# A hybrid mLSTM and DeltaNet decoder step: the scheduler plays the program with instruction times

## Chip, cores and metric

The kernel runs on one core of one Trainium2 chip. The metric is the device time of one execution in microseconds (us). TensorE, VectorE, ScalarE, GpSimd and SyncE each work through a queue of their own in order; the profile calls them PE, DVE, ACT, POOL and SP, and PEld is TensorE loading weights.

## What is computed

Two layers, each a token mixer and a dense MLP, both followed by a layer norm over `ALPHA * x + sublayer(x)`. The first mixer is an mLSTM, the second a gated DeltaNet. There is one new sequence of 512 tokens and 8 samples of 4 tokens, which start from given states; model width 1024, MLP width 4096.

```python
# mLSTM, per chunk of the sequence and head
s = einsum(q, k) * w_intra
num = s @ v + w_inter * (q @ C);  den = s.sum() + w_inter * (q @ n)
h = num / max(abs(den), exp(-m_t))
C = decay * C + einsum(w_k, k, v)
out = (sigmoid(o) * head_rms(h)) @ w_out
...
# gated DeltaNet: A = I + strict(kb k^T * decay), sol = A^-1 [v*beta, kb*exp(G)] = [u, w]
v_new = u - w @ S
o = qg @ S + attn @ v_new
S = gL * S + kdec^T @ v_new
out = (head_rms(o) * silu(z)) @ w_out
...
# MLP
square(relu(x @ w1)) @ w2
```

The state S runs through the chunks of the prompt, so a chunk's step needs the state that the chunk before it left.

## The kernel before

All activations lie transposed: features on the 128 partitions, the 512 + 32 = 544 tokens along the free axis, in two halves of 272. Every large product goes through `mm3` (its matmul is L194): float32 is emulated by three passes, hi*hi, hi*lo and lo*hi. A weight tile of 512 KB comes by a DMA on SyncE's queue (`wraw`), ScalarE copies it to the high part `wh` (L111) and VectorE subtracts for the low part `wl` (L112); there are two buffers of each. PSUM has banks under four tags: g (3, the projections), a (2), s (2, the recurrent steps) and t (1).

Work in the two mixers is cut into units of two heads. In the mLSTM a unit is projected (L194), scanned over four chunks of 128 tokens (`scan`: transposes and scores L742, L743; L757, L759 for the outputs; L762 for the state; `head_out` on VectorE and ScalarE, L706 to L722, normalises the heads; L735 transposes them), and per pair of units the samples are decoded (`decode`: L786 to L821, where L821 is 16 passes a unit, then L824 and the state updates L834). `gate_out` and `out` close a pair.

In the DeltaNet a unit is projected, prepared (L1075 to L1098), its triangular matrix inverted in small blocks (`invert`, L1163 to L1210, with blocks of VectorE's L1124 and L1126 in front), and scanned over four chunks. One chunk of `scan` is a chain: L1253 (state times keys and queries) on TensorE, L1256 on VectorE, L1264 on TensorE, L1266 on VectorE and L1268 on ScalarE, L1271 and L1280 on TensorE, L1274 and L1282 on VectorE, then `norm_heads` (L1225 to L1229) on ScalarE and VectorE, and L1242 transposes the result. `decode` (L1311 to L1396; L1367 multiplies by the samples' states) and `update` (L1411 and L1417 on GpSimd, L1424 on TensorE) do the samples; `gate_out` makes the gate `sgmz` (L1438), `out` projects.

The program is written as Python generators. In the DeltaNet three lanes (inversion, scan, decode with update) are advanced by one step after so many L194 passes of the projection, as the table PERIODS says, in the order of ORDER; in the mLSTM the order is ORDER_A.

```python
HP = 400
AHEAD = 300
ORDER_A = "p0 s0 p1 s1 d0 y0 p2 s2 p3 s3 w0 d1 y1 w1"
ORDER = "p0 p1 p2 p3 y0 w0 p4 p5 y1 w1 p6 p7 y2 w2 y3 w3"
PERIODS = {"p0": (3, 3, 4), "y0": (5, 5, 6), "p7": (3, 3, 6)}
```

The order in which the program is written is a priority and not yet the order on an engine. The tile framework's scheduler plays the program through: at each point it gives an engine, out of the instructions whose operands and buffers are ready in that play, the one with the highest priority. Weight loads are written as if they stood 300 instructions earlier (AHEAD, L184), the mLSTM's scan and decode 400 (HP, L869, L872). The order that comes out is fixed when the kernel is built; on the chip each engine follows it and waits on semaphores. It is set up in `kernel`:

## Time and profile before

| | us |
|---|---|
| median of 3 runs | 1852.68 |
| lowest, highest | 1843.46, 1853.33 |
| profiled execution, its own time | 1849.81 |
| its span, first to last instruction | 1847.9 |
| TensorE busy | 1764.1 (95%) |
| VectorE busy | 1033.4 (56%) |
| ScalarE busy | 830.8 (45%) |
| GpSimd busy | 221.8 (12%) |
| mean granted TensorE clock | 0.961 |

The mLSTM mixer lies at about 0 to 340 us, the first MLP at 350 to 690, the DeltaNet at 690 to 1455, the second MLP behind it. [...] A matmul that waits for a semaphore at the head of the queue can be inside another's modelled time, so busy is not the same as useful: in a stretch the number of passes tells more.

### The profile page before, as it was taken

What the parts mean: (1) busy time and instruction counts of PE and PEld (TensorE: products, weight loads), DVE (VectorE), ACT (ScalarE), POOL (GpSimd) and SP (SyncE); (2) the same over time, 40 slices, a digit from 0 to 9 for tenths busy, and PEclk for the clock granted to TensorE, in tenths of its full rate; (3) what the DMA queues carried; (4) which work ended last, traced back from release to release, by engine and by line L of the source; (5) the groups of instructions that cost most, each with busy time, mean ns of one, the idle gap of its engine ahead of it and who ended that gap; (6) DMA issues with size and microseconds to landing.
All of it is one profiled execution on the core that took longest, in us unless ns stands there. A gap on an engine that the chain in (4) does not pass through costs nothing.

```text
span 1847.9 us, 35864 instructions
## 1 busy us (share of the span) xinstructions
PE 1764.1 (95%) x14580; PEld 1693.1 (92%) x14580; DVE 1033.4 (56%) x2360; ACT 830.8 (45%) x1874; POOL 221.8 (12%) x441
## 2 busy tenths in 40 slices
PE   7999999999999999899899999999899999999997
PEld 7999998999999998889788989898799899999996
DVE  7554766432344377775763777576458643234436
ACT  6444355421243157665542764475245642134314
POOL 2000000000000001223515322511240000000000
PEclk9999999999999999898987999999689999999999
DMA  4131222222223221222413423331233222222321
GB/s 158 58 106 67 75 81 92 84 88 92 85 87 103 85 69 51 67 54 84 141 37 108 117 75 102 111 94 53 77 98 101 80 82 91 92 82 91 105 68 49
DMA packets 84293, 158.89 MB, mean 86 GB/s; under 512 B 37536, under 2 KB 41504, under 8 KB 83616
## 3 DMA queue, kind: packets, MB, share of 16 engines
q1 hardware_dynamic: 84128, 156.60, 27.3%
q8 instruction: 115, 1.88, 0.4%
q14 instruction: 50, 0.41, 0.1%
HBM read 140.51 MB, written 16.06 MB: 85 GB/s over the span
## 4 chain that ended last, share of the span: by engine, by line
PE 79%; DVE 9%; ACT 4%; DMA 3%; POOL 3%; issue 2%; SPq 0%; ACTq 0%; DVEq 0%; POOLq 0%
PE pg_t L194 38%; PE pm_s L194 12%; PE pm_a L194 12%; PE pm_s L1367 2%; POOL sst L1417 1%; PE pm_s L1424 1%; DVE lnt L380 1%; DVE lnt L381 1%; PE pm_a L1089 1%; PE pm_s L1253 1%; PE pm_s L1264 1%; PE pm_s L1271 1%; ACT wh L111 1%; DVE wl L112 1%; DVE XL L392 1%
## 5 line engine op out<-in xcount | busy, mean ns | idle before, releaser
L194 PE MATMUL pg_t<-XH,wh 128*128 128x272 f32 x1480 | 444.8, 301 | 7.2 <-DVE sgmz L1438 5.0
L112 DVE TENSOR_TENSOR wl<-wraw,wh 128x1024 fp32r<-128x1024 f32 x200 | 245.1, 1225 | 368.6 <-ACT wh L111 367.1
L194 PE MATMUL pg_t<-XH,wl 128*128 128x272 f32 x1480 | 438.6, 297 | 0.8 <-DVE wl L112 0.8
L194 PE MATMUL pg_t<-XL,wh 128*128 128x272 f32 x1480 | 438.4, 296 | 0.0
L111 ACT CAST wh<-wraw 128x1024 fp32r<-128x1024 f32 (+1 forms) x201 | 210.0, 1045 | 495.3 <-PE pg_t L194 245.4
L194 PEld LDWEIGHTS pg_t<-XH,wh 128*128 128x128 f32 x1480 | 285.6, 193 | 12.3 <-DVE sgmz L1438 5.9
L194 PEld LDWEIGHTS pg_t<-XL,wh 128*128 128x128 f32 x1480 | 285.6, 193 | 2.3
L194 PEld LDWEIGHTS pg_t<-XH,wl 128*128 128x128 f32 x1480 | 284.9, 193 | 2.8 <-DVE wl L112 1.7
L194 PE MATMUL pg_t<-h,wh 128*128 128x272 f32 x672 | 129.1, 289 | 0.0
L194 PEld LDWEIGHTS pg_t<-h,wh 128*128 128x128 f32 x672 | 105.7, 189 | 0.3
L1417 POOL TENSOR_SCALAR sst<-sst,glc 128x128 f32<-128x128 f32 x128 | 82.3, 659 | 153.5 <-DMA sst<-in_s 115.6
L194 PE MATMUL pg_t<-h,wl 128*128 128x272 f32 x336 | 97.0, 289 | 0.0
L194 PE MATMUL pm_a<-h,wh 128*128 128x272 f32 x496 | 95.3, 289 | 0.0
L194 PE MATMUL pm_s<-h,wh 128*128 128x272 f32 x496 | 94.9, 289 | 0.0
L396 DVE SCALAR_TENSOR_TENSOR XR<-XR,pg_t 128x272 f32<-128x272 f32 x118 | 51.2, 435 | 69.4 <-PE pg_t L194 68.9
L194 PE MATMUL pm_s<-XH,wh 128*128 128x272 f32 x288 | 84.3, 293 | 0.0
L194 PE MATMUL pm_s<-XH,wl 128*128 128x272 f32 x288 | 84.0, 292 | 0.0
L194 PE MATMUL pm_s<-XL,wh 128*128 128x272 f32 x288 | 83.9, 291 | 0.0
L194 PE MATMUL pm_a<-XL,wh 128*128 128x272 f32 x280 | 82.3, 294 | 0.9 <-DVE XL L392 0.8
L194 PE MATMUL pm_a<-XH,wh 128*128 128x272 f32 x280 | 82.3, 294 | 0.0
L194 PE MATMUL pm_a<-XH,wl 128*128 128x272 f32 x280 | 81.3, 290 | 0.0
L999 DVE SCALAR_TENSOR_TENSOR acc<-pre,cst,acc 128x568 f32<-128x568 f32 x96 | 76.8, 804 | 6.5 <-ACT acc L997 5.1
(572 smaller groups left out, 4066.2 us busy)
## 6 DMA issues: line engine op xcount, KB each, us to landing
wraw<-in_w SPq DMA_DIRECT2D x64, 512.0 KB, 3.5
wraw<-in_wb SPq DMA_DIRECT2D x48, 512.0 KB, 3.6
wraw<-in_w2a SPq DMA_DIRECT2D x32, 512.0 KB, 3.4
sst<-in_s SPq DMA_DIRECT2D x64, 256.0 KB, 3.1
wraw<-in_wa SPq DMA_DIRECT2D x24, 512.0 KB, 3.5
wraw<-in_w2b SPq DMA_DIRECT2D x24, 512.0 KB, 3.5
wraw<-in_wbo SPq DMA_DIRECT2D x16, 512.0 KB, 3.9
out_ss<-sst SPq DMA_DIRECT2D x32, 256.0 KB, 3.2
```

The costliest lines, as they stand in the source:

```text
L111: S.copy(hi, src)
L112: V.tensor_tensor(lo, src, r32(hi), op=ALU.subtract)
L194: T.matmul(ps, lhsT=wt[:, k, :], rhs=xt[k][:, HS[h]], start=first and k == 0 and q == 0, stop=last and k == n - 1 and q == 2,)
L380: V.tensor_tensor(t, x, rs, op=ALU.mult)
L381: V.tensor_tensor(t, t, mu, op=ALU.subtract)
L392: V.tensor_tensor(XL[j][:, HS[h]], x, r32(XH[j][:, HS[h]]), op=ALU.subtract)
L396: V.scalar_tensor_tensor(x, x, ALPHA if first else 1.0, ps, op0=ALU.mult, op1=ALU.add)
L999: V.scalar_tensor_tensor(acc, pre[:, q:q + WC], cw[q], acc, op0=ALU.mult, op1=ALU.add)
L1089: T.matmul(pk[:, q * 256:(q + 1) * 256], lhsT=kq[:, 0, c0:c0 + P], rhs=kq[:, :, c0:c0 + P], start=True, stop=True)
L1253: T.matmul(pks[:, w], lhsT=kq[:, w, cc], rhs=St, start=True, stop=True)
L1367: T.matmul(pkq[:, r], lhsT=t[:, r], rhs=kqf[:, :, o:o + 4], start=True, stop=True)
L1417: G.tensor_scalar(st[:, r], st[:, r], glc[:, bb:bb + 1], None, op0=ALU.mult)
```

## The change

One line: the scheduler is told to play the program through on a simulator of the time line, with a duration for each instruction, and not on its default one.

```diff
-    with tile.TileContext(nc) as tc:
+    with tile.TileContext(nc, schedule_with_timeline_sim=True) as tc:
         hybrid_kernel(tc, *args)
```

The GpSimd work for scaling, masks and copies in the delta-net's steps (L1411, L1417 and others) stands in both kernels. Every engine has the same instructions before and after: 13006 on TensorE, 2360 on VectorE, 1740 on ScalarE, 441 on GpSimd, 490 DMA issues on SyncE. 6876 of TensorE's stand at another place in its queue, 1893 of VectorE's, 337 of GpSimd's and 273 of SyncE's. The MLPs keep their order on TensorE, VectorE and SyncE; the mixers do not.

First place: TensorE in the mLSTM, the last chunk of unit 1's scan. `pm_s` are PSUM tiles of the recurrent steps, `pg_t` those of the projection, XH and XL the high and low part of the input. Before:

```order
L194 MATMUL pg_t_1427<-XL4_87,wh_1422 128x272
L194 MATMUL pg_t_1427<-XH4_79,wl_1423 128x272
L194 MATMUL pg_t_1427<-XH5_80,wh_1422 128x272
L194 MATMUL pg_t_1427<-XL5_88,wh_1422 128x272
L194 MATMUL pg_t_1427<-XH5_80,wl_1423 128x272
L194 MATMUL pg_t_1427<-XH6_81,wh_1422 128x272
L194 MATMUL pg_t_1427<-XL6_89,wh_1422 128x272
L194 MATMUL pg_t_1427<-XH6_81,wl_1423 128x272
L735 MATMUL pm_s_1199<-ident_129,ho_hn_1189 128x128 x2
L757 MATMUL pm_s_1204<-vtok_803,sw_1195 128x129
L759 MATMUL pm_s_1204<-cnp_219,qs_1197 128x129
```

After, from the chunk before to the same L757 and L759:

```order
L759 MATMUL pm_s_1165<-cnp_219,qs_1158 128x129
L762 MATMUL pm_s_1170<-vtok_803,kwz0_400 128x129 x2
L742 MATMUL pm_s_1191<-ident_129,kf_801 128x128
L743 MATMUL pm_s_1191<-qz1_403,kf_801 128x256
L735 MATMUL pm_s_1199<-ident_129,ho_hn_1189 128x128 x2
L757 MATMUL pm_s_1204<-vtok_803,sw_1195 128x129
L759 MATMUL pm_s_1204<-cnp_219,qs_1197 128x129
```

The L194 passes between L743 and L735 are gone from here; they stand ahead of the scan.

Second place: TensorE in the delta-net, the second chunk of unit 0's scan, from its L1264 (`rhs` times the inverse `X`) on. L1311 and L1319 belong to the decode, L1089 to L1098 to the preparation of unit 1. Before:

```order
L1264 MATMUL pm_s_8726<-rhs_8712,X_8370 128x128 x2
L1098 MATMUL pm_a_8921<-RRb_7840,hmr_136 128x256 x2
L194 MATMUL pg_t_9541<-XH3_78,wl_9475 128x272
L194 MATMUL pg_t_9541<-XH4_79,wh_9474 128x272
L194 MATMUL pg_t_9541<-XL4_87,wh_9474 128x272
L194 MATMUL pg_t_9541<-XH4_79,wl_9475 128x272
L1061 MATMUL pm_t_9467<-ident_129,acc_9456 128x128 x4
L1271 MATMUL pm_s_8742<-vd_8729,ktok_7930 128x256
L1311 MATMUL pm_s_8801<-blk_148,exprow_8796 128x4
L1095 LDWEIGHTS identb_134
L1095 MATMUL pm_a_8943<-maskw_144,identb_134 128x512
L1098 MATMUL pm_a_8943<-RRb_7840,hmr_136 128x256 x2
```

After:

```order
L1264 MATMUL pm_s_8726<-rhs_8712,X_8370 128x128 x2
L1271 MATMUL pm_s_8742<-vd_8729,ktok_7930 128x256
L1311 MATMUL pm_s_8801<-blk_148,exprow_8796 128x4
L1280 MATMUL pm_s_8811<-vn_8731,A_8155 128x128 x2
L1319 MATMUL pm_s_8849<-onesr_137,kqs_8847 128x1 x2
L1242 MATMUL pm_s_8866<-ident_129,go_on_8822 128x128 x2
L1253 MATMUL pm_s_8871<-St_8653,kq_7928 128x256 x2
L1264 MATMUL pm_s_8898<-rhs_8874,X_8370 128x128 x2
L1333 LDWEIGHTS identb_134
L1333 MATMUL pm_s_8905<-masks_145,identb_134 128x256
L1334 MATMUL pm_s_8905<-exprow_r_8798,onesr_137 128x256
L1271 MATMUL pm_s_8936<-vd_8901,ktok_7930 128x256
```

The next link follows with a decode pass or two between, and one chunk runs into the next (L1242, L1253) without a projection pass.

Third place: TensorE in the last unit's scan, from the second chunk (L1242) to the third, with the update's L1424. Before:

```order
L1242 MATMUL pm_s_16449<-ident_129,go_on_16430 128x128 x2
L1253 MATMUL pm_s_16454<-St_16252,kq_14478 128x256 x2
L194 MATMUL pg_t_16462<-XH4_79,wh_16378 128x272
L194 MATMUL pg_t_16462<-XL4_87,wh_16378 128x272
L194 MATMUL pg_t_16462<-XH4_79,wl_16379 128x272
L194 MATMUL pg_t_16462<-XH5_80,wh_16378 128x272
L194 MATMUL pg_t_16462<-XL5_88,wh_16378 128x272
L1264 MATMUL pm_s_16472<-rhs_16457,X_15505 128x128 x2
L194 MATMUL pg_t_16462<-XH5_80,wl_16379 128x272
L194 MATMUL pg_t_16462<-XH6_81,wh_16378 128x272
L1424 MATMUL pm_s_16493<-VM_16387,KM_16491 128x512
L1424 MATMUL pm_s_16493<-VM_16392,KM_16491 128x512
```

After:

```order
L1424 MATMUL pm_s_16440<-VM_16392,KM_16438 128x512
L1424 MATMUL pm_s_16440<-VM_16387,KM_16438 128x512
L1242 MATMUL pm_s_16449<-ident_129,go_on_16430 128x128 x2
L1253 MATMUL pm_s_16454<-St_16252,kq_14478 128x256 x2
L1264 MATMUL pm_s_16472<-rhs_16457,X_15505 128x128 x2
L1424 MATMUL pm_s_16493<-VM_16387,KM_16491 128x512
L1424 MATMUL pm_s_16493<-VM_16392,KM_16491 128x512
```

The projection's passes between the links have gone ahead of the scan; the update's passes stay.

## Rows read from the trace of the kernel before

**Rows 1.** The page: busy time by engine; granted clock in 40 slices, tenths.
```profile
PE 1764.1 (95%) x14580; PEld 1693.1 (92%) x14580; DVE 1033.4 (56%) x2360; ACT 830.8 (45%) x1874; POOL 221.8 (12%) x441
...
PEclk9999999999999999898987999999689999999999
```

**Rows 2.** Windows by stage: stretch, length, busy time (instructions) by engine, clock, DMA.
```profile
core 0: us, PE busy (x) PEld busy (x) DVE busy (x) ACT busy (x) POOL busy (x), PEclk, DMA share, GB/s
50.00:350.00 300.00, 294.62 (x2235) 281.63 (x2235) 177.15 (x450) 141.77 (x370) 0.22 (x2) 0.99 0.24 79
340.00:690.00 350.00, 347.34 (x2742) 345.36 (x2741) 149.32 (x224) 111.70 (x171) 0.78 (x2) 1.00 0.27 86
400.00:450.00 50.00, 50.00 (x402) 50.00 (x401) 13.39 (x17) 8.62 (x9) 0.00 (x0) 1.00 0.27 90
690.00:1455.00 765.00, 711.59 (x6403) 660.97 (x6403) 509.89 (x1341) 426.53 (x1085) 208.38 (x408) 0.92 0.29 85
```

**Rows 3.** TensorE's waits, whole span: us in total, times, longest us.
```profile
PE pm_a L1163 <- DVE DT L1155: 10.1, 7, 3.1
...
PE pm_t L1036 <- DVE kq L1003: 6.5, 1, 6.5
...
PE pg_t L194 <- DVE sgmz L1438: 5.0, 4, 1.9
...
PE pm_s L735 <- DVE ho_hn L722: 0.6, 3, 0.3
```

**Rows 4.** Windows, three mLSTM scan rounds of unit 1, L735 to L735.
```profile
86.30:90.50 4.20, 4.20 (x35) 4.01 (x34) 2.48 (x11) 1.62 (x9) 0.00 (x0) 1.00 0.00 0
90.50:95.50 5.00, 5.00 (x40) 4.78 (x39) 3.70 (x11) 4.10 (x13) 0.00 (x0) 1.00 0.33 101
95.50:99.40 3.90, 3.90 (x33) 3.78 (x32) 1.68 (x8) 1.62 (x9) 0.11 (x1) 1.00 0.02 9
```

**Rows 5.** Chain that ended last, around L821: start, us, what.
```profile
102.63 3.58 PE pm_s L821 x32
106.21 3.17 PE pg_t L194 x25
109.38 0.03 issue
```

**Rows 6.** Windows, two delta-net scan rounds: all engines, then L194 alone.
```profile
888.12:895.30 7.18, 6.24 (x40) 5.32 (x40) 6.31 (x20) 3.77 (x14) 2.92 (x5) 1.00 0.32 82
1300.37:1310.68 10.31, 7.37 (x22) 5.10 (x23) 7.80 (x32) 2.78 (x11) 0.00 (x0) 0.52 0.14 54
...
888.12:895.30 7.18, 2.68 (x19) 2.55 (x19) 1.00 0.32 82
1300.37:1310.68 10.31, 1.21 (x3) 0.79 (x3) 0.52 0.14 54
```

**Rows 7.** Windows, the five long starved stretches of the delta-net, and their sum.
```profile
869.80:877.40 7.60, 7.60 (x66) 7.09 (x66) 3.32 (x11) 5.17 (x14) 0.66 (x2) 1.00 0.11 35
927.40:946.00 18.60, 14.99 (x155) 13.14 (x155) 7.75 (x19) 9.64 (x25) 2.99 (x6) 0.69 0.09 29
985.80:1004.90 19.10, 15.33 (x254) 11.91 (x254) 4.83 (x13) 5.10 (x16) 13.67 (x26) 0.62 0.11 41
1300.40:1320.20 19.80, 16.86 (x65) 14.36 (x65) 10.15 (x45) 3.61 (x14) 0.00 (x0) 0.51 0.17 59
1339.30:1350.30 11.00, 11.00 (x131) 9.57 (x130) 2.33 (x7) 3.59 (x9) 3.93 (x8) 0.50 0.03 10
sum 76.10, PE 65.77 PEld 56.08 DVE 28.39 ACT 27.10 POOL 21.25; mean PE 13.15 PEld 11.22 DVE 5.68 ACT 5.42 POOL 4.25
```

**Rows 8.** Windows, first and last of 14 short starved stretches, and their sum.
```profile
723.30:731.70 8.40, 6.00 (x26) 4.93 (x27) 3.95 (x12) 5.68 (x19) 0.79 (x5) 0.75 0.04 8
...
1322.80:1328.20 5.40, 5.40 (x23) 5.17 (x24) 0.54 (x2) 0.40 (x1) 0.00 (x0) 0.50 0.28 60
sum 78.00, PE 71.26 PEld 63.28 DVE 37.78 ACT 33.47 POOL 20.95; mean PE 5.09 PEld 4.52 DVE 2.70 ACT 2.39 POOL 1.50
```

**Rows 9.** The page: subtraction and copy of a weight tile; its DMA's landing.
```profile
L112 DVE TENSOR_TENSOR wl<-wraw,wh 128x1024 fp32r<-128x1024 f32 x200 | 245.1, 1225 | 368.6 <-ACT wh L111 367.1
...
L111 ACT CAST wh<-wraw 128x1024 fp32r<-128x1024 f32 (+1 forms) x201 | 210.0, 1045 | 495.3 <-PE pg_t L194 245.4
...
wraw<-in_w SPq DMA_DIRECT2D x64, 512.0 KB, 3.5
```

## The prediction, made before the changed kernel ran

> **What bounds the kernel now.** I read the page first. TensorE is busy 95% of the span and the granted clock drops in a few slices only [rows 1]. Busy time alone does not tell where time is lost, since a matmul that waits for its operand at the head of the queue, or runs at half clock, is also counted as busy. So next the stretches. In the MLP 402 matmuls fill 50 us at full clock, so one weight pass of L194 costs 50/402 = 0.125 us when nothing holds it up. The mLSTM stretch (50 to 350 us) has TensorE idle for 5.4 of 300 us. The delta-net stretch (690 to 1455 us) has it idle for 53.4 of 765 us, at a mean clock of 0.92; with two levels, 0.5 and 1.0, that is 2 x 0.08 x 765 = 122 us at half clock [rows 2]. What can move in time is therefore mostly in the delta-net. There the waits are many and small, none over 10.1 us in total; they belong to the recurrent steps (inversion L1163, transposes L1036, the gate's sgmz; in the mLSTM the scan's L735) [rows 3].
>
> These steps are chains: TensorE, then VectorE or ScalarE, then TensorE again. The kernel hides them behind L194 passes of the next unit's projection, and the order on TensorE decides how many passes stand between two links. A link with many passes behind it costs nothing; a link with none costs its whole latency.
>
> **The change, part by part.** No instruction is added or dropped on any engine; names and counts are the same. The MLPs keep their order on TensorE, VectorE and SyncE, so I cost them at nothing: both stretches stay as they are (the first is busy 347.3 of 350 us [rows 2]). What remains is the order in the two mixers. I laid the TensorE orders of both kernels out by their work alone (each pass at the interval at which its kind is issued where nothing waits, as the 0.125 us above) and looked for stretches with hardly any L194 in them. The counts come from the orders, the prices from rows.
>
> *mLSTM, end of unit 1's scan and decode 0* (first order fence). Now 11 us of TensorE work have three L194 passes among them. (i) Two scan rounds keep only 1.90 and 1.54 us of TensorE work. The rounds of before last 3.9 to 5.0 us with TensorE full [rows 4], and L735 at their end waits 0.3 us at the longest [rows 3], so the chain of a round is near the shortest of them: 3.9-1.9 + 3.9-1.5 = +4.4 us. (ii) L824 now stands straight behind the 32 passes of L821. Before, 25 L194 stood between and took 3.17 us; L824 then waited 0.03 us [rows 5]. The same head-norm chain is now waited for: +3.2 us. (iii) The chain L786 to L818 loses its seven fillers and the L834 lose theirs, three behind each pair: +4 us, an estimate at 0.125 us a pass for some 30 passes. (iv) Decode 1 is drawn together in the same way (two L194 in 5.2 us of work): +4 us. (v) The other rounds stand looser; at most the 5.4 us of idle [rows 2] can go, most of it not theirs: -3 us. Sum +12.6, so +13 us; from 0, if the chains are shorter than their cover was, to +17, if nothing is given back.
>
> *Loads.* Two weight loads at the start of the second half get only 2.5 to 6 us of TensorE work as lead; landing, copy and subtraction take 3.5 + 1.05 + 1.23 = 5.8 us [rows 9]. So 0 to 3.3 us late; I take +3. The other loads keep their distance. On VectorE and ScalarE a step that now waits at the head of its queue holds up the split of the next weights (L111, L112) behind it; two weight buffers lie ahead of L194, so I cost this at nothing, and without that cover it is the 1.05 + 1.23 us of a split [rows 9]. The 273 places changed on SP's queue are state loads and stores with far more room. GpSimd's 337 changed places are state scalings, which the L1424 passes wait for; these passes move back with them, and I cost that at nothing. If that cover goes, each late scaling costs its wait in the update steps, which is part of the price per us below.
>
> *Delta-net, long starved stretches* (second and third order fence). Before has five stretches with over 5 us of TensorE work and almost no L194: 31.6 us of work that took 76.1 us, some 56 of them at half clock (twice the missing share of the clock by the length of each) [rows 7]. That is 44.5 us lost, 44.5/31.6 = 1.41 us per us of work. After has seven, with 8.1, 5.1, 17.3, 7.5, 8.9, 5.9 and 7.2 = 60.0 us of work. At the same price 60.0 x 1.41 = 84.6 us are lost: +40 us. The bounds are the cheapest stretch (7.6 us for 5.7 of work, at full clock: 0.33, so 20 us lost, -24) and the dearest (19.8 for 6.75, at clock 0.51: 1.93, so 116 us lost, +71) [rows 7]. I take the mean because the new stretches resemble the dear ones, inversion, update and scans with no projection, and not the cheap one. A second way to count agrees: seven of the 24 scan rounds (the time from one L1242 to the next) now hold only 21.4 us of TensorE work together. Of before, a round with 19 L194 took 7.18 us and one with three took 10.31 us [rows 6]; seven of these are 50 to 72 us, so +29 to +51.
>
> *Delta-net, short starved stretches* (2.5 to 5 us of work). Before has 14: 48.0 us of work in 78.0 us, 0.63 lost per us [rows 8]. After has six with 18.6 us of work. 29.4 us x 0.63 = -18 us, from 0 to -30.
>
> *Delta-net, the rest.* In the middle of the stage the links now stand 2 to 4 us apart (373 links in place of 145) where 0.25 to 2 us was usual. What this can give back is bounded by the idle that lies outside the listed stretches: 53.4 - 10.3 - 6.7 = 36.4 us [rows 2, 7, 8]. I take half, -18 us, with ends at 0 and -36; the other half is stage entries, such as the 6.5 us of L1036 [rows 3], which wait for work that no order brings forward.
>
> Sum: +13 +3 +40 -18 -18 = +20 us on the profiled run's 1849.8 us, **1869 us** in round numbers. The profiled run is 3 us under the median of 1852.7, well inside the spread of its three runs (1843 to 1853), so I make no correction.
>
> [...] The row: the 19.8 us from 1300 us on, with 65 matmuls in them, ran at clock 0.51, while the mLSTM rounds with 33 to 40 matmuls in 4 to 5 us ran at 1.00 [rows 4, 7]. [...]
>
> **The rivals.**
> A, *faster*: the new long stretches are no dearer than the short ones of before. For it: two or three chains (inversion, update, scan) alternate in the 17.3 us stretch, so one can hide another's latency. Against: the stretches of before at 1.66 to 1.93 also alternate chains, and the clock still fell there [rows 7]. At 0.63 per us, 60.0 x 0.63 = 38 us lost, -7 in place of +40, and the sum is 13+3-7-18-18 = -27: 1823 us. The point at which the sign turns is a price of 1.07.
> B, *no change*: the price is that of the fifth stretch, 11.0 us for 5.2 of work, 1.1 [rows 7]: 66 us lost, +22, and the sum is +2: 1852 us.
> C, *much slower*: every long stretch runs at half clock throughout, as the one at 1300 us did, and the middle gives nothing back. 13+3+71-18 = +69 with the price 1.93, 1919 us; with the credit of the middle 1901. For it: both dearest stretches are the ones at the lowest clocks. Against: the stretch at 869.8 us kept full clock with its fillers gone. [...]
> That the setting does nothing is excluded: 6876 of 13006 TensorE instructions stand elsewhere.
>
> **How the numbers follow.** Forecast (price 1.2 to 1.7) 0.45; A 0.27; B 0.18; C 0.10. The likeliest case gives 1869, its own range 1857 to 1887. Both signs hold much chance, so the range has to reach into A and C: 1822 to 1902 leaves out the far half of each. About 0.5%, 9 us, is what a measurement of this kernel can tell from no change. Faster by more than that: A and a bit of B, 0.29. Within: most of B and the low end of the forecast, 0.20. Slower: 0.51.
>
> **What would show it.** In the profile after: the slices with a low clock should be fewer in the first two thirds of the delta-net and deeper around seven places; windows on those places should show hardly any L194 and far more time than work. In the mLSTM, the step from L821 to L824 should show TensorE waiting for VectorE's L722 for about 3 us, and two rounds of unit 1 near 3.9 us with little in them. The waits of L1163 and L1242 should change places from many short ones to fewer long ones. I am wrong if the long stretches run at full clock with no idle, or if the delta-net stage ends earlier although they are idle, since then the middle gave back more than 36 us.

## The result, and the profile after

The changed kernel takes 1908.72 us (median of 4 runs, 1905.07 to 1913.4) against 1853.01 of the kernel before (1843.46 to 1860.44): a ratio of 1.0305, 95% interval 1.025 to 1.036. Slower, as forecast, but by 56 us where the forecast had 16, and 7 us above the range's upper end. The profiled run took 1913.4 us with a span of 1911.2 and a mean granted clock of 0.948.

First the page: busy time by engine and the granted clock in 40 slices, to be held against [rows 1].

```profile
PE 1777.7 (93%) x14580; PEld 1708.8 (89%) x14580; DVE 1039.0 (54%) x2360; ACT 827.8 (43%) x1874; POOL 244.5 (13%) x441
...
PEclk9989998999999999897879899998978999999998
```

TensorE's idle time grew from 83.8 to 133.5 us (span less busy), at the same work. In windows of 1 us over the span the granted clock reads 1.00 in 1689 of 1848 before and 0.50 in 130, and 1.00 in 1691 of 1911 after and 0.50 in 174; the few others lie between. From these two levels I estimate the time at half clock as twice the missing share of the clock by the span: it grew from 144 to 199 us, and two low digits lie ahead of the first MLP now, at decode 0 and at the norm.

Then the windows by stage, as in [rows 2] (length, busy time by engine, granted clock, share and rate of the DMAs):

```profile
50.00:385.00 335.00, 308.94 (x2276) 298.58 (x2276) 182.50 (x461) 145.52 (x384) 0.23 (x2) 0.95 0.21 71
385.00:725.00 340.00, 336.96 (x2669) 335.21 (x2668) 145.02 (x218) 104.88 (x156) 0.78 (x2) 1.00 0.28 89
725.00:1516.00 791.00, 715.81 (x6407) 664.08 (x6406) 505.77 (x1333) 420.57 (x1084) 228.88 (x408) 0.91 0.28 82
```

The surprise is in the first line. From 50 us to the first MLP it is now 335 us and not 300, with 26 us of idle in place of 5.4. The first MLP's first pass over its hidden layer `h` comes 34.9 us later than before, the second MLP's 60.5 us later.

To see where it goes finer than by windows, I took for each matmul the time to the next one, less the interval at which its kind is issued where nothing waits, and summed it by the stage of the program to which the late matmul belongs. These are sums over all 12960 matmuls of the two traces, in us:

| stage | before | after | more | forecast |
|---|---|---|---|---|
| start | 9.0 | 11.1 | 2.1 | 0 |
| mLSTM, projections, scans, decodes | 13.6 | 30.3 | 16.7 | 13 |
| norm behind the mLSTM, with `out` | 12.1 | 25.5 | 13.3 | 3 |
| first MLP and its norm | 6.8 | 9.0 | 2.2 | 0 |
| delta-net to the last unit's scan | 182.8 | 187.7 | 4.9 | 4 |
| end of the last scan, `out`, norm | 10.2 | 27.9 | 17.7 | in the 4 |
| second MLP and its norm | 4.6 | 8.6 | 4.0 | 0 |

Up to the last scan the mixers come out near the forecast. The rows with the four norms, which it took for free, hold 37 of the 61 us, the end of the last scan included. That row has two parts: behind the last L1242 (1406 us before, 1462 after), at `out` and the norm, it grew by some 9 us, and by about as much in the scan itself, which belongs to the forecast's delta-net.

The two mLSTM rounds of the first order fence (windows, from one L735 to the next, as [rows 4]):

```profile
110.10:115.00 4.90, 2.75 (x18) 1.98 (x18) 2.64 (x11) 1.62 (x9) 0.00 (x0) 1.00 0.00 0
115.00:118.90 3.90, 1.75 (x14) 1.55 (x14) 1.50 (x7) 1.62 (x9) 0.11 (x1) 1.00 0.00 0
```

They hold 18 and 14 matmuls where the three of before held 33 to 40, and last as long. Behind them comes decode 0 in the chain that ended last (start, us, what), against [rows 5]:

```profile
123.13 5.36 PE pm_s L821 x32
128.50 0.18 ACT ho_d L711
...
130.38 0.30 DVE ho_hn L722
130.73 0.33 PE pm_s L824
```

Where 25 passes stood between L821 and L824, the chain now runs over ScalarE and VectorE for 2.2 us. And L821 takes 5.36 us, not 3.58: the clock fell here, to a mean of 0.67 where it had been 1.00. The windows over L821, before and after:

```profile
102.63:106.21 3.58, 3.58 (x35) 3.58 (x34) 1.72 (x2) 0.00 (x0) 0.00 (x0) 1.00 0.02 5
...
123.13:128.49 5.36, 5.34 (x32) 5.14 (x31) 1.41 (x2) 0.00 (x0) 0.00 (x0) 0.67 0.00 0
```

The norm behind the mLSTM, TensorE's waits from 286 to 336 us (us in total, times, longest):

```profile
PE pm_a L194 <- ACT XH L391: 4.6, 1, 4.6
PE pg_t L367 <- DVE lnb L360: 3.5, 1, 3.5
PE pg_t L194 <- ACT wh L111: 2.7, 1, 2.7
PE pg_t L194 <- DVE wl L112: 2.1, 1, 2.1
```

and the chain there:

```profile
296.39 1.39 PE pg_t L194 x11
297.80 1.06 ACT wh L111
298.88 1.23 DVE wl L112
300.85 0.53 ACT lnb L373
301.40 0.44 ACT lnb L374
301.86 0.44 DVE lnb L376
302.30 1.05 DVE lnt L380 x3
304.06 1.06 DVE lnt L381 x3
```

Read it as a list of what stands ahead of the norm. L367 has delivered its sum at 296.4. Then come eleven projection passes, a weight copy and its subtraction, and only then the norm's L373; on VectorE three L380 go ahead of the first L381, so ScalarE's first copy is later still. TensorE has a share in this: the norm's second sum, L370, stands behind the same passes and starts 2.7 us after L367, where before it started 0.6 us after. The next weight tile, whose load was issued at 300.1 us, is copied at 307.5 only, behind the norm's copies on ScalarE; L194 waits for that copy (2.7 us) and its subtraction (2.1). In the second half the passes that stood behind L367 before have been used up, and L194 waits 4.6 us for the first normalised tile (L391).

The seven long starved stretches of the forecast, windows as [rows 7], first, longest, last and sum:

```profile
856.00:888.10 32.10, 22.16 (x92) 17.15 (x91) 19.27 (x76) 11.85 (x46) 2.57 (x4) 0.68 0.10 18
...
946.90:999.60 52.70, 36.99 (x352) 27.19 (x350) 28.70 (x90) 23.32 (x70) 25.72 (x43) 0.74 0.33 98
...
1439.20:1462.80 23.60, 15.63 (x65) 10.85 (x64) 11.19 (x26) 8.06 (x28) 7.66 (x13) 0.82 0.25 86
sum 169.60, PE 125.83 PEld 100.32 DVE 83.11 ACT 72.89 POOL 44.02; mean PE 17.98 PEld 14.33 DVE 11.87 ACT 10.41 POOL 6.29
```

60.0 us of work in 169.6 us: 1.83 lost per us, the dear end of the forecast's range (0.33 to 1.93) and not its mean of 1.41. Why the first stands alone, the timeline shows at its end (start, us, engine, line; in brackets the idle time before and what ended it):

```profile
886.72 0.39 ACT L987 COPY pre<-pg_t 128x272 f32<-128x272 f32 x1 [2.85 <-DVE kq L1003]
```

ScalarE empties a projection's PSUM bank here (L987), and the first projection pass behind the stretch needed that bank; its weights had been split at 847.5 us. The four transposes L1036 just ahead of it on TensorE waited for the same L1003 as L987. L987 itself waited for VectorE's L1003, whose inputs were ready at 847.1 us and which ran at 886.0, behind the scan's last round in VectorE's queue. L1003 writes `kq`, which has three buffers, and that round is the last to read the oldest. That the full ring of buffers put it there I conclude from the code; no run shows it, and a fourth buffer was not tried.

### The profile page after: what moved, and what is told of

The parts are those of the page before. It is cut to its first block, busy times and chain, and to the rows that moved or that the text cites. A ratio compares the mean times of both kernels' runs of the same rounds, so it can differ in the third digit from the quotient of the medians.

```text
span 1911.2 us, 35861 instructions
## 1 busy us (share of the span) xinstructions
PE 1777.7 (93%) x14580; PEld 1708.8 (89%) x14580; DVE 1039.0 (54%) x2360; ACT 827.8 (43%) x1874; POOL 244.5 (13%) x441
## 4 chain that ended last, share of the span: by engine, by line
PE 77%; DVE 11%; ACT 4%; DMA 3%; POOL 2%; issue 2%; SPq 0%; ACTq 0%; DVEq 0%; POOLq 0%
PE pg_t L194 38%; PE pm_s L194 12%; PE pm_a L194 12%; PE pm_s L1367 2%; POOL VM L1411 1%; DVE wl L112 1%; DMA out_ss<-sst 1%; DVE XR L396 1%; DVE acc L999 1%; PE pm_t L356 1%; PE pm_s L1253 1%; POOL sst L1417 1%; DVE lnt L380 1%; PE pm_a L1089 1%; ACT wh L111 1%
## 5 line engine op out<-in xcount | busy, mean ns | idle before, releaser
L194 PE MATMUL pg_t<-XH,wh 128*128 128x272 f32 x1480 | 445.1, 301 | 9.4 <-ACT wh L111 5.3
L194 PE MATMUL pg_t<-XH,wl 128*128 128x272 f32 x1480 | 440.5, 298 | 3.2 <-DVE wl L112 3.2
L194 PE MATMUL pg_t<-XL,wh 128*128 128x272 f32 x1480 | 440.1, 297 | 0.9 <-DVE XL L392 0.9
L194 PEld LDWEIGHTS pg_t<-XH,wh 128*128 128x128 f32 x1480 | 288.8, 195 | 12.2 <-ACT wh L111 5.9
L194 PEld LDWEIGHTS pg_t<-XH,wl 128*128 128x128 f32 x1480 | 287.7, 195 | 5.1 <-DVE wl L112 4.0
L194 PEld LDWEIGHTS pg_t<-XL,wh 128*128 128x128 f32 x1480 | 288.5, 195 | 2.8 <-DVE XL L392 1.3
L194 PE MATMUL pg_t<-h,wh 128*128 128x272 f32 x672 | 128.7, 288 | 0.0
L194 PEld LDWEIGHTS pg_t<-h,wh 128*128 128x128 f32 x672 | 105.6, 188 | 0.2
L194 PE MATMUL pg_t<-h,wl 128*128 128x272 f32 x336 | 96.9, 288 | 0.0
L1417 POOL TENSOR_SCALAR sst<-sst,glc 128x128 f32<-128x128 f32 x128 | 84.2, 676 | 85.8 <-DMA sst<-in_s 65.2
L194 PE MATMUL pm_a<-h,wh 128*128 128x272 f32 x496 | 94.4, 287 | 0.0
L194 PE MATMUL pm_s<-h,wh 128*128 128x272 f32 x496 | 94.3, 287 | 0.0
L194 PE MATMUL pm_a<-XH,wh 128*128 128x272 f32 x280 | 83.3, 297 | 8.2 <-ACT XH L391 6.8
L194 PE MATMUL pm_a<-XL,wh 128*128 128x272 f32 x280 | 83.4, 298 | 0.6 <-DVE XL L392 0.3
L194 PE MATMUL pm_s<-XH,wh 128*128 128x272 f32 x288 | 83.7, 291 | 0.0
L194 PE MATMUL pm_s<-XH,wl 128*128 128x272 f32 x288 | 83.4, 289 | 0.0
L194 PE MATMUL pm_s<-XL,wh 128*128 128x272 f32 x288 | 83.3, 289 | 0.0
L194 PE MATMUL pm_a<-XH,wl 128*128 128x272 f32 x280 | 82.5, 295 | 0.0
```

The lines of the kernel that those rows point to most:

```text
L194: T.matmul(ps, lhsT=wt[:, k, :], rhs=xt[k][:, HS[h]], start=first and k == 0 and q == 0, stop=last and k == n - 1 and q == 2,)
L1417: G.tensor_scalar(st[:, r], st[:, r], glc[:, bb:bb + 1], None, op0=ALU.mult)
```

## The experiments

Most of them fix the order on some engines. A kernel can do that with edges that order the issue but wait for nothing: the edit below goes behind the call of `hybrid_kernel`, and `chains` holds, for an engine or a stage, the instructions in the order that they have in the other kernel. All else is left to the scheduler.

```diff
         hybrid_kernel(tc, *args)
+        for q in chains:
+            for a, b in zip(q, q[1:]):
+                tc.add_manual_dep(b, a.name, no_sync, reason="chain")
```

**Is it TensorE's order?** The theory on entering was that of the forecast: TensorE's order alone, the other queues follow. Old TensorE order with the setting on:

> The setting is on, but TensorE's 12960 matmuls are chained in the order they had before; the other four engines take the order that the play with instruction times gives them under that. Theory (the order on TensorE alone makes the loss: projection passes run ahead of the chain steps they used to stand behind): 1845 to 1865 us. Rival (the loss comes from the other queues: splits, norm steps and loads in another order on VectorE, ScalarE and SyncE): over 1885 us.

The ratio is 1.0475 (1.0445 to 1.0506), 1938.07 us: with the old order on TensorE the kernel is slower than with the new one. The theory fell. The converse, the new TensorE order with the setting off:

> The converse: the setting is off, TensorE's matmuls are chained in the changed kernel's order, the other engines take the default play's order under that. Theory (TensorE's order): 1895 to 1920 us. Rival (the other queues): under 1870 us.

1983.46 us, 1.0716 (1.0688 to 1.0744), above both ranges. Both mixtures are slower than either kernel, so the orders of the queues belong together. TensorE's waits of the first say where (us in total, times, longest); L356 waited 4.0 us in all before:

```profile
PE pm_t L356 <- ACT lnt L352: 20.0, 8, 5.3
PE pm_s L1424 <- POOL VM L1411: 16.7, 4, 5.8
PE pm_s L1242 <- DVE go_on L1229: 11.6, 12, 1.9
```

**Holding the passes back.** The forecast's mechanism, passes that run ahead, was to be cured by a window (`pe` are TensorE's matmuls as written, `fill` and `passes` the L194 passes among them, `k` 150 or 60):

```diff
+    for i in pe:
+        if i.name in passes:
+            n += 1
+        elif n + k < len(fill):
+            tc.add_manual_dep(fill[n + k], i.name, no_sync, reason="window")
```

> The setting is on, and one edge is added for each matmul that is not an L194 pass: the L194 pass that is written 150 passes behind it may not be issued ahead of it. In the changed kernel the middle step has 242 passes written behind it issued ahead of it, in the one before 109. Theory (run-ahead of the passes starves the steps): a good half of the loss goes, 1855 to 1885 us. Rival (other queues, or the steps' chains are slow for another reason): stays at 1900 to 1915 us.

> As the run with 150, with a run-ahead of 60 passes (7.5 us) at most. Theory: the starved ends are gone and the even spacing in the middle stays, 1815 to 1850 us, under the kernel before. Rival (a step waits on TensorE's queue for its operand since no more passes can be taken ahead of it, so bounded run-ahead only moves the waiting): 1870 us or more.

1919.89 us (1.0372, 1.0337 to 1.0406) and 1964.78 (1.061, 1.058 to 1.0639). The orders changed as meant: with 150 passes one long starved stretch is left in the delta-net, not seven. The time did not fall; the rivals are nearer, the first by 5 us too low. The waits with 150 (in the changed kernel the first was 16.7 us, the second 6.7, the third did not occur):

```profile
PE pm_s L1242 <- DVE go_on L1229: 18.8, 11, 3.5
PE pm_s L1242 <- DVE xb L1126: 10.1, 3, 6.5
PE pm_s L1242 <- DVE tb L1124: 7.3, 3, 2.8
```

The step now stands at the head of TensorE's queue and waits for VectorE, where the inversion's small blocks (L1124, L1126) are queued ahead of what it needs, and the passes behind it wait with it. With six of its seven starved stretches gone, the delta-net with its last scan had only 3 us less of late matmuls than in the changed kernel; the mLSTM had 8 us more. So a starved stretch tells that a chain runs alone, but taking the starvation away was worth next to nothing here, since the chain stayed slow on the other queues.

**Which queue?** More engines were chained in the old order, setting on.

> The setting is on; TensorE's and VectorE's instructions are chained in the order they had before, ScalarE, GpSimd and SyncE take the play's order. With TensorE alone chained the time was 1938 us, 86 over the kernel before. Theory A (that 86 us is VectorE's queue: splits, the 15-step inversion and norm steps placed ahead of a step that TensorE waits for): under 1875 us. Theory B (ScalarE's or GpSimd's queue, whose waits L356 behind L352 and L1424 behind L1411 grew most): over 1900 us.

> As the run before, with ScalarE chained in its old order too; only GpSimd and SyncE are left to the play. Also the control for the chaining itself. Theory A and B alike: 1848 to 1862 us if GpSimd and SyncE don't matter and chains cost nothing; GpSimd's share of the loss shows as anything above that (the waits for L1411 grew by some 14 us).

| old order on | us | ratio, 95% interval |
|---|---|---|
| TensorE | 1938.07 | 1.0475 (1.0445 to 1.0506) |
| and VectorE | 1883.19 | 1.0169 (1.0131 to 1.0206) |
| and ScalarE | 1860.13 | 1.0037 (1.0016 to 1.0058) |
| none: the changed kernel | 1908.72 | 1.0305 (1.025 to 1.036) |

With TensorE's order held, the play's order on VectorE is worth 55 us, that on ScalarE 23, those on GpSimd and SyncE 7. Theory B put the loss on ScalarE's and GpSimd's side; the larger part is VectorE's, though 1883 lies between the two ranges. The third row also shows that chains cost next to nothing: with three engines chained the kernel is within 0.6% of before. Bear in mind that these are shares at TensorE's old order, and of orders that the play made under it: in the built programs 871 of VectorE's 2360 instructions would have to move to get from the first row's order to the changed kernel's. What VectorE's order costs in the changed kernel itself no run measures. Left free, TensorE's order gives 29 us back (1938 to 1909). GpSimd's order shows in the third row's run (L1424 waited 2.2 us for L1411 before) and costs little:

```profile
PE pm_s L1424 <- POOL VM L1411: 15.9, 4, 6.0
```

**The norms.** First by TensorE alone, at the norms behind the two mixers:

```diff
-            T.matmul(p1, lhsT=ones, rhs=s1, start=True, stop=True)
+            self.sums = T.matmul(p1, lhsT=ones, rhs=s1, start=True, stop=True)
...
-                first = projs([w1[layer, m] for m in range(4)], extra) if f == 0 else []
+                with tc.issue_after(prev.sums.ins):
+                    first = projs([w1[layer, m] for m in range(4)], extra) if f == 0 else []
```

> The changed kernel with one rule: the first MLP passes behind a mixer's layer norm may not be issued ahead of the norm's last sum (L367 of the second half), as it was in the kernel before. Theory (at the two joins, which cost 12 and 9 us more than before, these passes had been used up ahead of the norm and left the second half's norm uncovered): 1886 to 1898 us. Rival (the joins are slow by VectorE's and ScalarE's order): 1905 to 1915 us.

1930.67 us, 1.0415 (1.0376 to 1.0454): slower than the changed kernel and above both ranges. The passes now stand behind L367, but the sum of squares (L356) still comes after it, and the stage at the first norm costs 28.7 us where it cost 25.5. The wait only moved to an earlier place, L356 behind L352. Most of the 22 us over the changed kernel, some 16, are late matmuls of the delta-net.

Then with the old relative order at all four norms, on three engines and on VectorE and ScalarE alone:

> The changed kernel; only at the four layer norms (the steps from the last output projection to the first MLP or delta-net passes) the instructions of TensorE, VectorE and ScalarE are chained in the relative order they had before. The loss by stage of the program puts 38 of the 61 us more on these four places. Theory (at the norms the new order on the three queues is the loss): 1870 to 1885 us. Rival (the loss there is only handed on from the stage ahead and comes back elsewhere): 1900 us or more.

> As the run before, but only VectorE and ScalarE are chained at the norms, TensorE is left to the play. Theory A (it is VectorE's and ScalarE's order there, splits and the next half's work ahead of the norm's chain): within 6 us of the run before. Theory B (TensorE's order there, passes used up ahead of the norm): 1898 to 1912 us.

1911.12 us (1.0314, 1.028 to 1.0348) and 1911.54 (1.0321, 1.0289 to 1.0353): no gain by either. The first run's rival holds; the second's time fits both of its theories, so the stages must tell them apart. By stage the first norm was mended with three engines, 14.0 us in place of 25.5, and its waits are those of the kernel before (284 to 330 us):

```profile
PE pm_t L356 <- ACT lnt L352: 1.8, 2, 1.2
PE pm_a L194 <- DVE XL L392: 0.8, 3, 0.4
PE pm_a L367 <- DVE lnb L360: 0.6, 1, 0.6
```

With VectorE and ScalarE alone it fell to 21.8 only: their old order gave back 3.7 us, TensorE's on top of it 7.8. But the loss came back elsewhere. The norm behind the first MLP, whose first steps my chain had left out, lost 7 us more than in the changed kernel; the delta-net 8; the mLSTM 4, though ahead of the norm the order on TensorE and VectorE had not changed, so that much is most likely a difference between executions (the profiled one was 5 us above its median). So the new order at the norm, on all three engines, is what costs there, and mending it at one place does not mend the time: the play gave the delta-net, which was not chained, another order than the changed kernel's.

**The gate's buffers.** Two lines, `bufs=2` to `bufs=3`, for the tile `vf` of the mLSTM's values and gates:

> The changed kernel with three buffers in place of two for the tile that holds the mLSTM's values and gates. Theory (the gate's passes ran ahead until two gate tiles and PSUM's three banks were full, so the rest of the scan and the decode, which must free them, stood alone: 17 + 5 us): with a third tile passes are left for the decode, 1885 to 1897 us. Rival (the steps stood alone since the play gives them the first place whenever they are ready): 1905 to 1915 us. With the setting off a third tile leaves the order of every engine as it is.

1904.17 us, 1.0272 (1.0226 to 1.0318), not to be told from the changed kernel by its interval, and next to the rival's range. The place reacted all the same as the theory says: the mLSTM's late matmuls fell from 30.3 to 22.2 us, with 11.6 us off the end of unit 1's scan and decode 0 and 3.5 added elsewhere, and no starved stretch over 5 us is left there in TensorE's order. The delta-net fell by 10 us without having been touched, the first norm rose by 3 (the profiled run, 1895.4 us, was the fastest of the four). Both together:

> The old order at the four norms and three value and gate buffers together. By stage the third buffer took 12 us from the scan's end and the decode of the mLSTM. Theory (the two losses are separate and add up): 1855 to 1873 us. Rival (as the buffer alone, whose median fell by 4 us only): 1875 us or more.

1906.37 us, 1.0281 (1.0244 to 1.0317). The two don't add up; the rival holds.

**Where, by halves.** The delta-net alone left to the new play, all else in the old order on three engines; and the converse.

> Setting on; everything outside the delta-net stage (both MLPs, the mLSTM, the four norms, the output projection at the end) is chained in the old order on TensorE, VectorE and ScalarE; the delta-net is left to the new play. Theory (the new order outside the delta-net makes most of the loss, that in the delta-net about 5 to 15 us with its end): 1858 to 1875 us. Rival (the loss is the delta-net's, and the stages ahead of it only hand it on): 1885 us or more.

> The converse: only the delta-net is chained in the old order on the three engines, the rest is left to the new play. Theory: the mLSTM's 19 us and the norms' 20 to 30 us stay, 1885 to 1902 us. Rival (the delta-net's): under 1875 us.

1880.84 us (1.0154, 1.012 to 1.0188) and 1905.58 (1.0286, 1.0257 to 1.0315). With the old delta-net, 52 of the 56 us stay. The larger part is outside the delta-net, as the theory has it, but each run lies 4 to 6 us above its bound, and the delta-net costs 28 us, not 5 to 15; 28 and 52 are more than 56, so the halves don't simply add up. The two runs' stages, more than before, beside the changed kernel's:

| stage, us more than before | changed | delta-net alone new | delta-net alone old |
|---|---|---|---|
| mLSTM | 16.7 | -0.1 | 17.0 |
| norm behind it | 13.3 | 4.1 | 13.4 |
| first MLP and its norm | 2.2 | 3.5 | 1.5 |
| delta-net | 4.9 | 27.6 | 4.7 |
| end of the last scan, norm | 17.7 | 2.9 | 9.3 |

The mLSTM's and the first norm's loss stay to a few tenths when the delta-net is put back. The delta-net's is not as steady: entered from the old order it costs 28 us (in a profiled run that was 10 us above its median), in the changed kernel 5. Over the kernels that leave the delta-net to the new play without a window, its late matmuls run from 178 us (three gate buffers) to 210 (this one), against 183 before, with edits far ahead of it; part of that lies between executions, as the profiled one with three buffers was 9 us under its median. The +5 is one draw of this spread.

**The hand-set priorities.** One finding needed no chip: with the norm's steps written at priority HP, the setting on gives the same order on every engine, word for word; likewise AHEAD at 150 or 300, and HP at 0 or 400 on TensorE. With the setting off these edits move instructions. So is the loss what the priorities were worth? The edits are the norm's steps at HP, and one or both of these lines:

```diff
-HP = 400
-AHEAD = 300
+HP = 0
+AHEAD = 0
...
-                ln.feed(j, h)
+                with tc.high_priority(offset=HP):
+                    ln.feed(j, h)
```

> The kernel before, setting off, with the norm's sums and steps written with the priority 400 that the mLSTM's scan has. The same edit with the setting on leaves the order of every engine word for word as it is, with it off 22 of TensorE's, 72 of VectorE's and 12 of ScalarE's instructions move. Theory (the norms of the kernel before lose little to order): 1846 to 1858 us; the joins there cost 27 us in all, so at most 10 us are to be had.

> The kernel before, setting off, with the mLSTM's priority of 400 for scan and decode set to 0. With the setting on, 0 and 400 give the same order on TensorE. Theory (the new play loses because it makes this priority void): the mLSTM's 19 us appear here too, 1865 to 1875 us. Rival: 1848 to 1860 us.

> Setting off, with both priorities set by hand at 0: scan and decode, and the weight loads (300). Theory (the new play's loss is what these two were worth): 1885 to 1915 us. Rival (they are worth little, and the new play's order is worse for another reason): under 1870 us.

> Setting off, the weight loads written without their priority of 300, the mLSTM's 400 kept. Theory (the gain of the run without both is the loads', since the run with the mLSTM's alone at 0 gave 0.2%): 1838 to 1850 us, all of it in the delta-net, where the rest fell by 11 us. Rival (it takes both): 1850 to 1860 us.

> Setting on, both priorities at 0. Theory (the loss is the new play's ranking by its own instruction times): 1895 to 1920 us as the changed kernel. Rival (the priorities and the instruction times get in each other's way): under 1880 us.

| setting | priorities | us | ratio, 95% interval |
|---|---|---|---|
| off | norm's steps at 400 too | 1850.61 | 0.9987 (0.9962 to 1.0013) |
| off | HP 0 | 1849.7 | 0.9976 (0.9957 to 0.9995) |
| off | HP 0, AHEAD 0 | 1844.6 | 0.9933 (0.9899 to 0.9966) |
| off | AHEAD 0 | 1845.79 | 0.9954 (0.9929 to 0.998) |
| on | HP 0, AHEAD 0 | 1927.71 | 1.0387 (1.0344 to 1.043) |

No: without them the kernel before is no slower, so this theory fell. Without both it is even faster, 0.7% under the kernel before. The gain lies in the delta-net, 182.8 to 171.9 us of late matmuls, and comes with the loads' priority alone. In the run without both the transposes wait much less for `kq` than before (6.5 us):

```profile
PE pm_t L1036 <- DVE kq L1003: 1.2, 1, 1.2
```

With the setting on, doing without them does not help: 1927.71 us is 8 above the theory's range and far from the rival's. The loss is not what the priorities were worth. That leaves the new play's own ranking; which of its choices cost, no run takes apart.

## Why the prediction was half right

**Sign and first-named place: right.** The first order fence was read as two rounds that would each last about 3.9 us with nothing in them, and L824 waiting some 3 us. They lasted 4.9 and 3.9, and the wait was 2.2 us. Of the waits that were to become fewer and longer, L1163's nearly went away and L1242's became more (before, then after):

```profile
PE pm_a L1163 <- DVE DT L1155: 10.1, 7, 3.1
PE pm_s L1242 <- DVE go_on L1229: 2.8, 4, 1.5
...
PE pm_s L1242 <- DVE go_on L1229: 16.7, 11, 2.5
...
PE pm_a L1163 <- DVE DT L1155: 0.2, 1, 0.2
```

**mLSTM, +13 forecast, +16.7 measured.** The credit of 3 for looser rounds did not come (the other rounds changed by less than 2 us), and the half clock over decode 0, L821 at 5.36 us in place of 3.58, stood in no term. A slip besides: the parts without the credit add up to 15.6, not to the upper end of 17.

**"The MLPs keep their order ... so I cost them at nothing" and, of VectorE and ScalarE, "so I cost this at nothing": the steps that failed.** A norm belongs to neither an MLP nor a mixer in my sum, and I looked at stretches poor in L194 on TensorE alone, where a norm does not show. At the norms the chain runs through three queues, and other work now stands ahead of it on each: projection passes between its two sums on TensorE, splits and the other half's steps on ScalarE and VectorE. By the table the sum missed 41 of the 61 us: some 25 at the four norms (10 behind the mLSTM beyond the 3 for the loads, 9 behind the last scan, 6 in the rows of the other two), 10 in the delta-net with its last scan, 4 in the mLSTM, 2 at the start. The splits, costed at nothing, made L194 wait 2.7 and 2.1 us at the first norm alone. Which engine it is depends on where one asks: at the first norm TensorE's old order gave back 7.8 us and VectorE's with ScalarE's 3.7; over the whole program, with TensorE's old order held, VectorE's queue was worth 55 us and ScalarE's 23. And since the time stayed at 1911 us with the first norm mended, the norms are where the loss shows; that they are its cause is not shown.

**Delta-net, +4 forecast: too low by some 10 us with its last scan, and not shown in the terms.** The +5 of the table stops short of the last scan, whose stretch (1439.2 to 1462.8 us) was among the seven that I had priced; with the 9 us there it is +14. By the same stretches as in the forecast, the loss in the seven long ones was 169.6-60.0 = 110 us against 84.6 (the price was 1.83, not 1.41). The short ones and the rest fell by some 45 us in all where I had 36. So the terms were off on both sides by 10 to 25 us, and that they nearly cancelled up to the last scan is luck. The mechanism behind them did worse: the run with a window of 150 had one of the seven stretches left and was as slow. A starved stretch marks where a chain runs alone, but the price per us of it is not a cost that can be taken out.

**The rival that came nearest** was C, every long stretch at half clock and 1901 to 1919 us. Its time was right and its price nearly (1.83 against 1.93), but its condition was not: the seven stretches ran at 0.52 to 1.00, one of them near half clock throughout, and a good part of the missing time was at the norms. The reason given for it, that both dearest stretches are the ones at the lowest clocks, misread a row: the lowest clock, 0.50, belongs to the 11.0 us stretch, at a price of 1.1. The windowed runs interleave more than the changed kernel and are no faster (1919.89 and 1964.78 us against 1908.72), so less interleaving is not shown to be what costs.

**What stays open.** Why the delta-net under the new play costs between 178 and 210 us of late matmuls depending on edits far ahead of it; why the end of the last scan still lost 18 us with its norm's order mended, though 9 with the old delta-net ahead of it; what VectorE's order costs at the changed kernel's own order on TensorE; and which of VectorE's moved instructions cost most. No run separates these.

## What to carry to other kernels

When a scheduler's way of ranking changes, compare the order on every engine that a critical chain runs through, not on the busiest one alone: here, with TensorE's order held, those of VectorE and ScalarE were together worth 78 us. Put the short serial joins between stages (a norm, the end of a scan) into the sum as stages of their own. And test hand-set priorities again after each such change: one that is kept here costs 0.5%, and under the new ranking other values (150 for 300, 0 for 400) left TensorE's order as it was.

## What was not expected of the hardware

The granted clock fell in a stretch that had run at 1.00 before. In the two rounds ahead of decode 0 TensorE was busy 2.75 of 4.90 and 1.75 of 3.90 us, at a clock of 1.00; in the decode behind them, where no projection pass stands, it was 0.50 from 119.9 to 126.7 us, and the 32 passes of L821 took 5.36 us at a mean of 0.67, where they took 3.58 before.
